# The PSUM bank of the gate's spatial mix in a hybrid decoder trunk: from the bank pair `pt` to the bank `tq`

## The chip, the cores and the metric

The kernel runs on one core of one Trainium2 chip. The metric is device time in microseconds (us) of one execution of the whole program, median of several runs. The core has five engines with a queue of instructions each: TensorE (PE in the profile; PEld is its weight load), VectorE (DVE), ScalarE (ACT), GpSimd (POOL) and SyncE (SP), which here only issues the transfers between device memory and the on-chip memory. Each engine runs its queue in order and waits at an instruction whose inputs or whose output buffer are not ready. TensorE writes its results into PSUM, a memory of eight banks of 512 float32 columns by 128 partitions; VectorE and ScalarE read them from there.

## The reference, cut to what matters

Two residual layers over 1024 tokens of width 1024. Layer 0 mixes the tokens with a spatial gate (A) and a dilated attention (B) side by side; layer 1 uses a gated linear attention; both end with a gated MLP. The change touches the gate of layer 0:

```
def chunked_gmlp(u, v, ln_g, ln_b, w_s, b_s):
    Bn, S, _ = u.shape
    nc = S // A_CHUNK                       # chunks of 128 tokens
    vn = layer_norm(v, ln_g, ln_b).reshape(Bn, nc, A_CHUNK, A_GROUPS, A_GROUP_DIM)
    causal = jnp.tril(jnp.ones((A_CHUNK, A_CHUNK), dtype=bool))
    ws = jnp.where(causal[None], w_s.astype(jnp.float32), 0.0)
    mixed = jnp.einsum('gts,bnsgc->bntgc', ws, vn) + b_s.astype(jnp.float32).T[:, :, None]
    return u.astype(jnp.float32) * mixed.reshape(Bn, S, A_WIDTH)

    # in even_mixer, h the normed input, z = h @ w_in split into u, v, q, k, vb
    a_out = chunked_gmlp(gelu(u), gelu(v), a_ln_g, a_ln_b, a_ws, a_bs)
    # b_out: three dilated attention branches of 8 heads over q, k, vb
    return concatenate([a_out, b_out], -1) @ w_out
```

## The kernel before

The 1024 tokens are eight tiles of 128. Every large product is made of float32r matmuls of 128x512, each value split into a high and a low part and three of the four partial products taken, so that one output tile of 128 tokens by 512 columns costs 8 x 3 = 24 matmuls (`mm_tok`, line 183, `PASSES`, line 41).

Layer 0 runs as follows. For each of four pairs of heads, `project` (line 776) makes queries, keys and values, and `unit` (line 750) makes one block of attention: scores on TensorE into the bank tag `sc` (line 741), mask and row minimum on VectorE (line 746), exp on ScalarE (line 747), transposes of the probabilities on TensorE into the tag `pt` (line 761, tiles `pP`), a copy to `pT` on ScalarE or VectorE (lines 764 and 766), and the product with the values into the tag `po` (line 769). `project` also transposes keys and queries into the tag `tq` (lines 821 to 828, tiles `tk` and `tq`). `dilated` (line 850) makes eight units per pair (tiles `sc3d`, `pP3d`, `po3d` for the last pair). `combine` and `combined` (lines 867 to 892) join the branches and write the result to device memory (`bcat`), after a round trip of the dilated part through device memory (`od`, then `on`).

After the last pair, `gmlp` (line 656) projects v (tiles `pv0` to `pv7`, lines 698 and 651) into two tiles `mx0` and `mx1` of four token tiles each, applies gelu (line 676) and layer norm (lines 679 to 688), and mixes along the tokens: for each half and each pair of groups one PSUM tile `pm` gets two float32 matmuls of 128x256 (line 692), and VectorE adds the bias while it moves `pm` back into `mx` (line 694). There are eight such tiles, `pm00` to `pm06` and `pm10` to `pm16`. `u_proj` (line 701) projects u (tiles `pu0` to `pu7`), applies gelu on ScalarE (line 705) and multiplies the result into `mx` (line 706). While `pu7` is made, before the matmuls of its last two slices, `turn` (line 714) transposes the first token tile for the output projection, four blocks of `mx0` and four of `cat00`, which is read back from `bcat` (line 711); the transposes go into two `pt` tiles `pc00` and `pc01` (line 720), from which ScalarE and VectorE make the two parts of `hq` (lines 101, 102). The output projection (`out_first`, line 446, tiles `po00`, `po01`, ...) reads `hq` and weights `wo`, split on ScalarE and VectorE (lines 101, 102). The second token tile is transposed at line 456 (`pc10`, `pc11`).

The eight banks of this stage are given out by tag (line 526): `pt` 2, `sc` 2, `pj` 2 (the projections), `po` 1, `tq` 1. The tiles of a tag take its banks in turn, in the order in which the program asks for them; a tile waits until the tile that held its bank has been read.

The order in each queue is not the program's: a scheduler (`schedule_with_timeline_sim`, line 1380) sorts the instructions of each engine by its own estimate of times, within the data and buffer dependencies. A handful of instructions are pinned (`keep_in_program_order`), among them the first transpose of `turn` and the first step of `combine`. The change of a bank therefore moves instructions on every engine.

Of the kernel before, what the change touches and what calls it, by code (L numbers as in the profile page):

```python
# [9 lines left out]
F32 = mybir.dt.float32  # L10
# [9 lines left out]
P = 128  # L20
# [27 lines left out]
def flat(t):  # L48
    return t.rearrange("p a b -> p (a b)")
# [7 lines left out]
def trunk(ctx: ExitStack, tc: tile.TileContext, a, out):  # L57
# [72 lines left out]
    def load_half(src, name, gains=None):  # L130

        return [w for kp in range(4)
                for w in load_w(src[kp], f"{name}{kp}", gains=None if gains is None else gains[:, 2 * kp : 2 * kp + 2])]
# [4 lines left out]
    def inv_rms(ssq, cols, n, name, r=None):  # L138
        if r is None:
            r = small.tile([P, cols], F32, tag="rs%d" % cols, name=name)  # L140
        G.tensor_scalar(r, ssq, 1.0 / n, EPS, op0=ALU.mult, op1=ALU.add)  # L141
        G.tensor_tensor(r, r, mhalf[:, :cols], op=ALU.pow)
        return r
# [506 lines left out]
    def proj512(ps, ws, name, consume, amid=None):  # L650
        for n in range(NT):
            pj = ps.tile([P, 512], F32, tag="pj", name=f"{name}{n}")
            mm_tok([(pj, slice(0, 512))], lambda k: tok(n, k), lambda k: ws[k], KD, amid if n == NT - 1 else None)
            consume(n, pj)

    def gmlp(ps, gm):

        wv = load_half(a["w_vu"][0], "wv", g0)
        lnG = gm.tile([P, 512], F32, name="lnG")
        Q.dma_start(lnG, a["ln_g"].partition_broadcast(P))  # L660
        lnB = gm.tile([P, 512], F32, name="lnB")
        Q.dma_start(lnB, a["ln_b"].partition_broadcast(P))
        bs = gm.tile([P, GROUPS], F32, name="bs")
        Q.dma_start(bs, a["a_bs"])
        ws = gm.tile([P, GROUPS, P], F32, name="ws")
        Q.dma_start(ws, a["a_ws"])

        G.affine_select(out=ws, in_=ws, compare_op=ALU.is_ge, fill=0.0, base=0,
                        pattern=[[0, GROUPS], [1, P]], channel_multiplier=-1)

        def consume(n, pj):
            half, j = n // 4, n % 4
            A.activation(mx[half][:, j, :], pj, AF.Copy, scale=r0[:, n : n + 1])
            if j < 3:
                return
            ge = A.activation(flat(mx[half]), flat(mx[half]), AF.Gelu)
            if half:
                tc.keep_in_program_order(ge)
            for j in range(4):
                gv = mx[half][:, j, :]  # L680
                st = small.tile([P, 6], F32, tag="bn", name=f"bn{half}{j}")
                V.bn_stats(st, gv)
                mv = small.tile([P, 2], F32, tag="mv", name=f"mv{half}{j}")
                V.bn_aggr(mv, st)
                r = inv_rms(mv[:, 1:2], 1, 1, f"lr{half}{j}")
                V.tensor_scalar(gv, gv, mv[:, 0:1], r, op0=ALU.subtract, op1=ALU.mult)
                V.tensor_mul(gv, gv, lnG)
                V.tensor_add(gv, gv, lnB)
            for g in range(0, GROUPS, 2):
                pm = ps.tile([P, 2, 4, 64], F32, tag="pt", name=f"pm{half}{g}")  # L690
                for i in range(2):
                    T.matmul(pm[:, i], ws[:, g + i, :], mx[half][:, :, (g + i) * 64 : (g + i) * 64 + 64],
                             start=True, stop=True)
                V.tensor_tensor(mx[half][:, :, g * 64 : g * 64 + 128].rearrange("p n (i c) -> p i n c", i=2), pm,
                                bs[:, g : g + 2, None, None].to_broadcast([P, 2, 4, 64]), op=ALU.add)

        mx = [gm.tile([P, 4, 512], F32, name=f"mx{h}") for h in range(2)]
        proj512(ps, wv, "pv", consume)
        return [mx[n // 4][:, n % 4, :] for n in range(NT)]

# [224 lines left out]
    def odd(ps, narrow, rl):  # L925

        with tc.tile_pool(name="T", bufs=1, reuse_waits="tile") as tp, \
                tc.tile_pool(name="gl", bufs=2, reuse_waits="tile") as gl:
            return gla(ps, narrow, gl, [tp.tile([P, 2, 4, 512], F32R, name=f"Tm{i}") for i in range(3)], rl)
# [284 lines left out]
    def banks(st, **bufs):  # L1214
        return Tagged({t: st.enter_context(tc.tile_pool(name="psf_" + t, bufs=b, space=PSUM, reuse_waits="tile"))
                       for t, b in bufs.items()})

    def narrow():
        pss.close()
        return banks(pss, m1=5, pt=3)  # L1220
# [4 lines left out]
    ps = banks(pss, mm=3, pt=2)  # L1225
    for l in range(2):
        w_out = a["od_w_out" if l else "ev_w_out"]
        x_in = (lambda n: x2[n]) if l else (lambda n: rows(a["x"], n))
        with ExitStack() as ops:
            if l == 1:  # L1230
                ps, last = odd(ps, narrow, ops.enter_context(tc.tile_pool(name="rl", bufs=1, side="right", reuse_waits="tile")))
# [29 lines left out]
        with tc.tile_pool(name=f"T{l}", bufs=1, reuse_waits="tile") as tp:  # L1261
            T3 = [tp.tile([P, 2, 4, 512], F32R, name=f"T{l}{i}") for i in range(3)]
            if l == 0:
                ps = narrow()
# [4 lines left out]
        ps = banks(pss, mm=3, pt=2)  # L1269
# [114 lines left out]
```

## Time and profile before

| what | value |
|---|---|
| median of 3 runs | 2152.41 us (2152.16 to 2153.36) |
| the profiled execution's own time | 2150.36 us |
| its span, first to last instruction | 2147.9 us |
| TensorE matmul busy | 2120.8 us, 99% of the span |
| VectorE, ScalarE, GpSimd busy | 1512.2, 1035.8, 478.8 us |
| mean granted TensorE clock | 0.999 |
| first and last matmul of `pm` | 333.6 and 358.8 us |
| first and last VectorE step of line 694 | 334.6 and 359.5 us |

The profile is of one execution. A row of the timeline gives the start in us, how long the group of instructions lasted, the engine, the line of the kernel, the operation, the tile it writes and the tiles it reads, how many there were, and in brackets how long the engine had been idle and what ended that. Matmul ends are modelled, so rows of TensorE overlap by a fraction of a microsecond; the chain of waits cuts the same time into pieces that don't overlap (start, length, engine, line, count). TensorE's busy time leaves 27 us of the span; a change that moves nothing but waits can win at most that, and what lies in a stretch of lowered clock.

### The profile page before, as it was taken

The numbers are of one execution on the slowest core, as the hardware profiler recorded it, in microseconds if no ns is written. First come the engines' busy times: TensorE is split into PE (matmuls) and PEld (weight loads), VectorE is DVE, ScalarE is ACT, GpSimd is POOL, SyncE is SP. The second block draws the span as 40 slices with busy tenths as digits, with TensorE's granted clock in tenths as the row PEclk, the third lists the DMA queues.
The fourth block names the chain that finished last, engine by engine and source line by source line (L and its number), as shares of the span: only waits on it lengthen the run. The fifth ranks groups of instructions, "written<-read, shape, count | busy, mean of one in ns | idle before, by whom it ended". The sixth has DMA issues, their size and how long they took to land.

```text
span 2147.9 us, 29582 instructions
## 1 busy us (share of the span) xinstructions
PE 2120.8 (99%) x10380; PEld 1797.3 (84%) x10380; DVE 1512.2 (70%) x2436; ACT 1035.8 (48%) x2014; POOL 478.8 (22%) x521
## 2 busy tenths in 40 slices
PE   8999999999999999999999999999999999999999
PEld 7999987878888888878889888888788888888887
DVE  7466654576978878655576877677788888785554
ACT  7555664264444444444454455535544444444443
POOL 6344310013424335000020011011234324220000
PEclk9999999999999999999999999999999999999999
DMA  7022313754444544765553233386555544458664
GB/s 274 25 75 68 114 45 109 250 197 148 157 167 162 167 149 155 253 238 195 199 188 123 73 107 99 132 306 212 177 167 162 169 150 156 163 172 290 214 217 165
DMA packets 159701, 353.69 MB, mean 165 GB/s; under 512 B 17424, under 2 KB 54544, under 8 KB 159168
## 3 DMA queue, kind: packets, MB, share of 16 engines
q1 hardware_dynamic: 159408, 351.68, 48.6%
q8 instruction: 81, 1.33, 0.3%
q14 instruction: 68, 0.56, 0.1%
q10 hardware_dynamic: 144, 0.13, 0.0%
HBM read 243.15 MB, written 108.59 MB: 164 GB/s over the span
## 4 chain that ended last, share of the span: by engine, by line
PE 87%; DVE 4%; DMA 3%; ACT 3%; issue 1%; POOL 0%; SPq 0%; DVEq 0%; ACTq 0%
PE pgB L293 11%; PE puB L293 11%; PE pv L193 6%; PE pgC L293 6%; PE puC L293 6%; PE pdB L405 5%; PE pj L193 5%; PE pdC L405 5%; PE po L193 4%; PE pdO L405 4%; PE puA L293 3%; PE pgA L293 3%; PE pdP L405 2%; PE pdQ L405 2%; PE pu L193 2%; PE pBq L1084 2%
## 5 line engine op out<-in xcount | busy, mean ns | idle before, releaser
L102 DVE TENSOR_TENSOR da<-ar,da 128x512 fp32r<-128x512 f32 x154 | 106.2, 690 | 155.6 <-ACT da L101 155.3
L101 ACT CAST da<-ar 128x512 fp32r<-128x512 f32 x154 | 95.9, 623 | 212.5 <-PE pdC L405 98.5
L193 PE MATMUL po<-wo,hq 128*128 128x512 f32 x768 | 185.1, 397 | 1.5 <-DVE hq L102 1.2
L193 PEld LDWEIGHTS po<-wo,hq 128*128 128x128 f32 x768 | 142.7, 189 | 31.8 <-DVE hq L102 2.4
L193 PE MATMUL pv<-wv,hq 128*128 128x512 f32 (+2 forms) x768 | 140.0, 339 | 0.0
L405 PE MATMUL pdB<-dw,da 128*128 128x512 f32 x528 | 135.5, 391 | 1.3 <-ACT u L310 0.7
L405 PE MATMUL pdC<-dw,da 128*128 128x512 f32 x528 | 135.1, 390 | 0.0
L193 PEld LDWEIGHTS pv<-wv,hq 128*128 128x128 f32 x768 | 119.1, 189 | 14.7
L193 PE MATMUL pj<-wq,hq 128*128 128x384 f32 x576 | 118.5, 344 | 0.0
L405 PEld LDWEIGHTS pdB<-dw,da 128*128 128x128 f32 x528 | 98.7, 188 | 22.7 <-ACT u L310 1.1
L405 PEld LDWEIGHTS pdC<-dw,da 128*128 128x128 f32 x528 | 99.0, 188 | 20.5
L102 DVE TENSOR_TENSOR dw<-wr,dw 128x512 fp32r<-128x512 f32 x154 | 105.6, 686 | 10.2 <-ACT dw L101 9.7
L259 POOL TENSOR_TENSOR S1g<-rg 128x512 f32<-128x512 f32 x20 | 29.4, 1468 | 373.6 <-DMA wsd<-D 262.4
L141 POOL TENSOR_SCALAR rn<-ssq 128x1 f32<-128x1 f32 x24 | 9.3, 389 | 447.2 <-ACT h L149 244.1
L405 PE MATMUL pdO<-dw,da 128*128 128x512 f32 x396 | 102.2, 389 | 0.2 <-DVE dw L102 0.2
L101 ACT CAST dw<-wr 128x512 fp32r<-128x512 f32 x154 | 95.0, 617 | 11.4 <-DMA wr<-in_w_dn 6.7
L193 PEld LDWEIGHTS pj<-wq,hq 128*128 128x128 f32 x576 | 98.2, 188 | 0.2
L405 PEld LDWEIGHTS pdO<-dw,da 128*128 128x128 f32 x396 | 74.2, 188 | 16.0 <-DVE dw L102 0.6
L324 DVE SCALAR_TENSOR_TENSOR t<-g,cw,t 128x1022 f32<-128x1022 f32 x44 | 73.8, 1677 | 0.1
L308 DVE TENSOR_TENSOR g<-g,s1g 128x512 f32<-128x512 f32 x22 | 15.2, 693 | 79.9 <-ACT s1g L307 79.9
L323 DVE SCALAR_TENSOR_TENSOR t<-g,cw,t 128x1023 f32<-128x1023 f32 x44 | 56.2, 1278 | 16.1 <-ACT t L322 16.1
L259 POOL TENSOR_TENSOR S4u<-ru,S2u 128x512 f32<-128x512 f32 x20 | 48.9, 2447 | 54.6 <-DVE wg2p L102 9.6
(1084 smaller groups left out, 5410.3 us busy)
## 6 DMA issues: line engine op xcount, KB each, us to landing
ar<-actd SPq DMA_DIRECT2D x70, 512.0 KB, 3.6
rd<-in_w_down SPq DMA_DIRECT2D x44, 512.0 KB, 3.7
wsd<-D SPq DMA_DIRECT2D x88, 256.0 KB, 2.6
rg<-in_w_gate SPq DMA_DIRECT2D x42, 512.0 KB, 3.7
ru<-in_w_up SPq DMA_DIRECT2D x42, 512.0 KB, 4.8
wr<-wsd SPq DMA_DIRECT2D x40, 512.0 KB, 4.5
actd<-t SPq DMA_DIRECT2D x66, 256.0 KB, 2.3
wr<-in_w_dn SPq DMA_DIRECT2D x30, 512.0 KB, 4.7
```

What stands on the lines that cost most here:

```text
L101: (hi or A.copy)(dst[0], src)
L102: (lo or V.tensor_sub)(dst[1], src, f32(dst[0]))
L141: G.tensor_scalar(r, ssq, 1.0 / n, EPS, op0=ALU.mult, op1=ALU.add)
L193: T.matmul(o, L[i], R[jj][:, sl], start=(k == 0 and (ii, jj) == PASSES[0]), stop=(k == nk - 1 and (ii, jj) == PASSES[-1]))
L259: G.tensor_tensor(sums[name], x, y, op=op)
L293: mm = T.matmul(o, L[ii][:, j * P : j * P + P], right[p][:, jj, j, :], skip_group_check=more, start=(not more and j == 0 and (ii, jj) == P ...
L308: V.tensor_add(C22, C22, s1)
L323: V.scalar_tensor_tensor(t[:, 1:], g[:, : S - 1], w(1), t[:, 1:], op0=ALU.mult, op1=ALU.add)
L324: V.scalar_tensor_tensor(t[:, 2:], g[:, : S - 2], w(0), t[:, 2:], op0=ALU.mult, op1=ALU.add)
L405: T.matmul(o, L[ii][:, t * P : t * P + P], R[jj], skip_group_check=more, start=start and not more and (ii, jj) == PASSES[0], stop=stop and ...
L1084: T.matmul(o, L[ii][:, j * P : j * P + P], right[p][:, jj, j, :], skip_group_check=more, start=(not more and j == 0 and (ii, jj) == PASSES ...
```

## The change

The PSUM tile `pm` of the spatial mix is asked for under the tag `tq` (one bank) instead of `pt` (two banks). Nothing else in the text changes; the same matmuls and VectorE steps run.

```
             for g in range(0, GROUPS, 2):
-                pm = ps.tile([P, 2, 4, 64], F32, tag="pt", name=f"pm{half}{g}")
+                pm = ps.tile([P, 2, 4, 64], F32, tag="tq", name=f"pm{half}{g}")
                 for i in range(2):
                     T.matmul(pm[:, i], ws[:, g + i, :], mx[half][:, :, (g + i) * 64 : (g + i) * 64 + 64],
                              start=True, stop=True)
```

In `pt` the first `pm` comes behind the `pP` tiles of all attention units, since they were asked for earlier. In `tq` it comes behind the last `tq` tile of the last `project`. The order on each engine changes as follows; numbers behind a tile's name tell apart tiles of one name.

TensorE, in the projection of v (`pv6`, `pv7`) between the units of the last pair:

```order
 L193 MATMUL pv6_4109<-wv2_0_3871,hq01_86 128x512 x3
+L692 MATMUL pm00_4041<-mx0_3894,ws_3891 128x256 x2
 L193 MATMUL pv6_4109<-wv2_1_3874,hq11_88 128x512 x3
 L193 MATMUL pv6_4109<-wv3_0_3879,hq01_86 128x512 x3
 L193 MATMUL pv6_4109<-wv3_1_3882,hq11_88 128x512 x3
 L193 MATMUL pv7_4135<-wv0_0_3855,hq01_86 128x512 x3
```

`pm00` stood in the projection `pu4`, behind the transposes of the last unit; now it stands in `pv6`, six projections earlier, between two units. The other seven follow one by one, the last, `pm16`, in `pu4` (before: in `pu7`). The last unit's product with the values (`po3d1`) now has seven tiles `pm` ahead of it instead of one, and eight matmuls of `pu4` instead of 23.

TensorE, at the end of the projection of u and the start of the output projection:

```order
 L720 MATMUL pc00_4501<-ident_73,mx0_3894 128x128 x2
-L193 MATMUL pu7_4482<-wu3_0_4244,hq01_86 128x512 x3
-L193 MATMUL pu7_4482<-wu3_1_4247,hq11_88 128x512 x3
 L720 MATMUL pc00_4501<-ident_73,cat00_4450 128x128 x2
 L720 MATMUL pc01_4508<-ident_73,mx0_3894 128x128 x2
 L720 MATMUL pc01_4508<-ident_73,cat00_4450 128x128 x2
-L456 MATMUL pc10_4581<-ident_73,mx0_3894 128x128 x2
-L456 MATMUL pc10_4581<-ident_73,cat01_4577 128x128 x2
-L456 MATMUL pc11_4588<-ident_73,mx0_3894 128x128 x2
-L456 MATMUL pc11_4588<-ident_73,cat01_4577 128x128 x2
+L193 MATMUL pu7_4482<-wu3_0_4244,hq01_86 128x512 x3
+L193 MATMUL pu7_4482<-wu3_1_4247,hq11_88 128x512 x3
```

The last six matmuls of `pu7` moved behind all eight transposes of `turn`, and the eight transposes of the second token tile moved away from here, into the last matmuls of `po00`.

VectorE, at the end of `combined` and the splits of the output weights `wo`:

```order
 L891 TENSOR_TENSOR ot3n0_3073<-ot3n0_3073,on30_3849 128x4x128
 L891 TENSOR_TENSOR ot3n4_3376<-ot3n4_3376,on31_3851 128x4x128
-L694 TENSOR_TENSOR mx1_3895<-pm14_4210,bs_3889 128x2x4x64
+L706 TENSOR_TENSOR mx1_3895<-mx1_3895,ut5_4447 128x512
+L706 TENSOR_TENSOR mx1_3895<-mx1_3895,ut6_4479 128x512
 L102 TENSOR_TENSOR wo00_0_4547<-wo00r_4545,wo00_0_4547 128x512
 L102 TENSOR_TENSOR wo00_1_4550<-wo00r_4545,wo00_1_4550 128x512
-L694 TENSOR_TENSOR mx1_3895<-pm16_4214,bs_3889 128x2x4x64
 L102 TENSOR_TENSOR wo01_0_4555<-wo01r_4553,wo01_0_4555 128x512
-L706 TENSOR_TENSOR mx1_3895<-mx1_3895,ut4_4419 128x512
-L706 TENSOR_TENSOR mx1_3895<-mx1_3895,ut5_4447 128x512
-L706 TENSOR_TENSOR mx1_3895<-mx1_3895,ut6_4479 128x512
```

No step of line 694 is left behind the first step of `combine`; of the gate's products (line 706) three instead of four stand behind `combined`, two of them ahead of the splits. On ScalarE the number of table loads is the same. On SP two transfers behind the first four of `cat` change places (`wo13r` and `cat03`), nothing else.

More of the change, by code (lines that the diff above doesn't have):

```diff
@@ L689, in consume @@
             for g in range(0, GROUPS, 2):
-                pm = ps.tile([P, 2, 4, 64], F32, tag="pt", name=f"pm{half}{g}")
+                pm = ps.tile([P, 2, 4, 64], F32, tag="tq", name=f"pm{half}{g}")
                 for i in range(2):
```

## The prediction

> **What bounds the kernel now.** I read the page first.
>
> ```profile
> span 2147.9 us, 29582 instructions
> PE 2120.8 (99%) x10380; PEld 1797.3 (84%) x10380; DVE 1512.2 (70%) x2436; ACT 1035.8 (48%) x2014; POOL 478.8 (22%) x521
> ```
>
> TensorE is busy all but 27.1 us of the span, so the change, which removes no matmul, can win only TensorE's waits and its slow matmuls. The second view is the list of TensorE's waits, for the stage that the change touches.
>
> ```profile
> PE pc L456 <- DMA cat<-bcat: 1.3, 1, 1.3
> PE po L193 <- DVE hq L102: 1.2, 1, 1.2
> PE pP3d L761 <- ACT sm3d L747: 0.6, 1, 0.6
> PE pc L720 <- DMA cat<-bcat: 0.2, 1, 0.2
> ```
>
> Third, TensorE's timeline shows where they lie: one in the attention units of the last pair, three in a row between the projection of u and the output projection.
>
> ```profile
> 322.18 0.44 PE L761 MATMUL pP3d<-ident,sm3d 128*128 128x128 f32 x2 [0.60 <-ACT sm3d L747]
> ...
> 360.84 0.38 PE L720 MATMUL pc<-ident,mx 128*128 128x128 f32 x2
> 360.98 1.64 PE L193 MATMUL pu<-wu,hq 128*128 128x512 f32 x6
> 362.87 0.44 PE L720 MATMUL pc<-ident,cat 128*128 128x128 f32 x2 [0.25 <-DMA cat<-bcat]
> ...
> 365.22 0.44 PE L456 MATMUL pc<-ident,cat 128*128 128x128 f32 x2 [1.26 <-DMA cat<-bcat]
> ...
> 367.33 7.31 PE L193 MATMUL po<-wo,hq 128*128 128x512 f32 x24 [1.24 <-DVE hq L102]
> ```
>
> The last row holds more than a wait: the first 24 matmuls of the output projection take 7.31 us. The chain of waits has the eight transposes of the next token tile (0.87 us) and the next 24 matmuls, and the table of stretches has the granted clock (columns: stretch, length, busy time and count of PE, PEld, DVE, ACT, POOL, then PEclk, DMA share, GB/s).
>
> ```profile
> 374.64 0.87 PE pc L456 x8
> 375.52 5.49 PE po L193 x24
> ```
> ```profile
> 364.00:366.00 2.00, 0.78 (x6) 0.64 (x6) 2.00 (x5) 1.18 (x3) 0.00 (x0) 1.00 0.78 273
> 366.00:367.00 1.00, 0.09 (x1) 0.00 (x0) 1.00 (x3) 0.77 (x2) 0.00 (x0) 1.00 0.94 266
> 368.00:369.00 1.00, 1.00 (x3) 0.74 (x3) 1.00 (x2) 0.00 (x0) 0.00 (x0) 0.50 1.04 426
> 371.00:372.00 1.00, 1.00 (x6) 0.81 (x6) 0.00 (x0) 0.00 (x0) 0.00 (x0) 1.00 1.00 410
> ```
>
> TensorE did 0.87 us of work in the 3 us from 364 to 367; then its clock stood at 0.50 and three matmuls instead of six fitted into 1 us. So this stage loses 0.60 + 0.25 + 1.26 + 1.24 = 3.35 us in waits and 7.31 - 5.49 = 1.82 us at half clock, 5.17 us together. VectorE is full from 364 to 367 (2.00 of 2.00, 1.00 of 1.00): a queue of work stands there, and `hq`, for which the output projection waits, is at its end.
>
> **The change part by part.** Removed and added work: none. The same 16 matmuls and 8 VectorE steps run, at the same price. What changes is where they stand, and four things follow.
>
> (1) The wait of 0.60 us. ScalarE did two table loads and a gelu between the two exps of one unit:
>
> ```profile
> 318.23 1.28 ACT L705 ACT_TABLE_LOAD   x1
> 319.52 0.69 ACT L705 ACTIVATE ut<-pu,r 128x512 f32<-128x512 f32 x1
> 320.23 1.28 ACT L747 ACT_TABLE_LOAD   x1
> ```
>
> 1.28 + 0.69 + 1.28 = 3.25 us. In the new order of ScalarE this unit's two exps stand side by side ahead of `ut1`. Another unit, the last, now has table load, `ut2`, table load between its exps; TensorE has there a `po3d` product, six and more matmuls and a `pm` in between. I take 0 for it and 0.6 us, the old wait, as the upper bound. Gain 0.60, low end 0.
>
> (2) The transfer `cat`. It ends a chain that starts with the last attention product, and whether TensorE waits for it depends on both.
>
> ```profile
> 339.53 1.78 PE pm L692 x8
> ```
>
> Two `pm` are eight pieces on TensorE; one costs 1.78 / 2 = 0.89 us, one 512-wide matmul 5.49 / 24 = 0.229 us. The last `po3d` product has six more `pm` ahead of it (+5.34) and 15 fewer matmuls (-3.43), and the wait of (1) is gone (-0.60): it comes 1.3 us later. From there the chain runs through every engine:
>
> ```profile
> 339.57 0.59 ACT L861 COPY ot3d<-po3d 128x512 f32<-128x512 f32 x1 [5.16 <-PE po3d L769]
> ```
> ```profile
> 342.45 1.34 SPq L901 DMA_DIRECT2D on<-od  x2
> ```
> ```profile
> on<-od SPq DMA_DIRECT2D x2, 264.0 KB, 3.2
> ```
> ```profile
> 347.31 1.29 DVE L706 TENSOR_TENSOR mx<-mx,ut 128x512 f32<-128x512 f32 x2
> 348.52 0.68 DVE L694 TENSOR_TENSOR mx<-pm,bs 128x512 f32<-128x512 f32 x1
> 349.12 0.15 DVE L872 TENSOR_TENSOR cM<-ot3n,on 128x8 f32<-128x8 f32 x1
> 349.19 1.28 DVE L706 TENSOR_TENSOR mx<-mx,ut 128x512 f32<-128x512 f32 x2
> 350.39 0.16 DVE L875 TENSOR_TENSOR cE<-cM,ot3n 128x8 f32<-128x8 f32 x1
> ...
> 354.75 0.68 DVE L694 TENSOR_TENSOR mx<-pm,bs 128x512 f32<-128x512 f32 x1
> ```
>
> The first `on` has landed at about 342.45 + 3.2 = 345.65 us, yet `combine` (L872) starts at 349.12: 3.5 us behind the gate's steps in VectorE's queue, then 1.2 us more for two products between L872 and L875, and 0.6 us for one step of L694 inside `combined`. In the new order these stand ahead of the chain, at times when VectorE has nothing else, or behind it. The chain then goes 5.3 us faster and starts 1.3 us later; I take off another 0.5 us, since the second `on` lands 1 us behind the first and its half of L872 waits for it. Before, `cat` was there at 362.87 us (TensorE's wait ends); now at 362.87 - 5.3 + 1.3 + 0.5 = 359.4 us. TensorE comes to its first transpose of `cat` at 360.84 - 0.60 + 2 x 0.11 = 360.5 us (0.87 / 8 = 0.11 a transpose), as the same `pm` and `pu` matmuls are behind it. The cover is thus 1.1 us, and it has to hold, because the last six matmuls of `pu7`, which hid 1.4 us of that wait before, now stand behind it. The second token tile (`pc1`), whose wait was the 1.26 us, is now transposed behind 19 matmuls of `po00`, 4.4 us after its start. Gain 0.25 + 1.26 = 1.51; with the chain as long as before the wait comes back (first rival).
>
> (3) The wait for `hq`. VectorE reached it late:
>
> ```profile
> 366.60 2.47 DVE L102 TENSOR_TENSOR hq<-pc,hq 128x512 fp32r<-128x512 f32 x4
> ```
>
> In the new order the queue ahead of `hq` is one step of L706 and six splits of `wo` after `pu6` ends, some 0.7 + 7 x 0.6 = 4.9 us, each step at its distance in that queue (four steps of `hq` in 2.47 us); TensorE meanwhile does the 24 matmuls of `pu7` and eight transposes, 5.5 + 0.9 = 6.4 us. One step of `hq` later, at 5.6 us, `po00` may start: 0.8 us of cover. Gain 1.24; low end 0.4 less.
>
> (4) The half clock. It followed 3 us with 0.87 us of matmuls; with (2) and (3) gone TensorE has no such stretch. Gain 1.82, all or nothing. [...]
>
> (5) One bank instead of two. The next `pm` may be written only when L694 has read the last one:
>
> ```profile
> L694 DVE TENSOR_TENSOR mx<-pm,bs x8: 676/687/692, 334.6 to 359.5; 128x512 f32<-128x512 f32 x8
> ```
>
> Side by side, eight tiles in one bank would cost up to 7 x 0.69 = 4.8 us of waiting. But in the new order at least ten 512-wide matmuls stand between two `pm`, 2.3 us and more. I take 0. [...]
>
> Sum: 0.60 + 1.51 + 1.24 + 1.82 = 5.17 us. The profiled execution took 2150.36 us (span 2147.9 and 2.5 around it), 2.05 below the median of the runs; a gain of whole waits carries over to the median: 2152.41 - 5.17 = 2147.2 us. Against the low ends (0.6 and 0.4 less) it is 2148.2.
>
> What is late next: the stage behind waits again, the two longest times here:
>
> ```profile
> 437.72 1.53 PE L163 MATMUL pt<-ident,xt 128*128 128x128 f32 x12 [0.65 <-DVE xt L153]
> 470.95 2.79 PE L293 MATMUL pgB<-hq,wg0p 128*128 128x512 f32 x11 [1.31 <-DVE hq L102]
> ```
>
> These hang on VectorE and transfers that start from the third tile of the output projection, so they should move forward with it.
>
> **The rivals.** *A, the transfer chain is not shorter.* If `cat` takes as long as before (339.57 to 362.87, 23.3 us) from a start 1.3 us later, it is there at 364.2 us; TensorE, which now has nothing else to do, waits 3.7 us, does six transposes and six matmuls (0.65 + 1.37) and starts `po00` at 366.2 instead of 367.33, but with the eight transposes of `pc1` (0.87) still to do. Gain 0.3 us, or 2.1 with full clock: 2150.3 to 2152.1. For it: it is the longest chain here, and my cover is 1.1 us; against: the VectorE rows that leave it.
>
> *B, the half clock stays*, because something else made it or because a wait that is left is enough for it. Gain 3.35: 2149.1 us. For it: nothing in the rows; against: it follows the three waits at once. [...]
>
> *C, the gain is given back.* The two rows above wait for VectorE. If its work and the transfers there keep their own time, these waits grow by what was won: 2152.4 us. Against it: that work starts from TensorE's results in the output projection.
>
> *D, slower: the one bank stops TensorE.* The place is `pm14` in `pu3`. Its bank is freed by L694 of `pm12`, on VectorE behind the product with `ut2` (L706), which ScalarE makes between table loads. Fifteen matmuls of 512 columns stand between `pm12` and `pm14`, 3.4 us, less 0.69 for L694 itself: 2.7 us of slack. Each further microsecond stops TensorE, and the last unit with it; beyond 2.7 + 5.17 = 7.9 us of delay the kernel is slower than before, and beyond 12 us by over 0.2%. The nearest rows are those of (1): a load, a gelu and a load in the way are 3.25 us, which would cost 0.6 us. Four such delays would be needed: 2153 to 2157 us.
>
> **How the numbers follow.** The whole gain: 0.60. A: 0.20; B: 0.06; C: 0.09; D: 0.05. A change of 0.2% is 4.3 us, about what a measurement of this kernel can tell from none. The whole gain passes it if no more than 0.9 us of new waits comes with it; I give that nine in ten: faster 0.54. A, B, C and the rest of the first make 0.41 within 0.2%; D makes 0.05. The range holds the first case with its bounds (1.2 us to the far side for waits further on that shrink too), B and most of A: 2146.0 to 2152.0. The likeliest case alone: 2146.0 to 2148.6.
>
> **What would show it.** Right: no wait over 0.3 us for `cat` or `hq` between 355 and 370 us; PEclk at 1.00 through the first 24 `po` matmuls, which then last about 5.5 us apart from the transposes among them; L872 within 1 us of the landing of `on`; `po00` starting near 362.5 us. Wrong: a wait of `pc00` for `cat` of over 1 us (A), PEclk at 0.50 near 365 us without it (B), waits of over 3 us between 430 and 485 us (C), a wait of `pm` for L694 (D).

## The result and the profile after

| kernel | median, us | runs |
|---|---|---|
| before, measured beside it | 2152.90 (2150.25 to 2154.76) | 8 |
| after | 2146.55 (2145.40 to 2150.18) | 8 |

The ratio is 0.9975, interval 0.9965 to 0.9986: some 5.4 us less (3.0 to 7.5), where 5.17 were forecast. The ratio is not the quotient of the two medians, which is 0.9971, 6.35 us less. The profiled execution of after took 2149.18 us (span 2146.4), second longest of its eight runs. One execution of the third measurement of after, below, took 2979.05 us at a granted clock of 0.665, and every number given leaves it out.

The page of after has the same work in it as the page of before.

```profile
span 2146.4 us, 29574 instructions
PE 2121.5 (99%) x10380; PEld 1798.0 (84%) x10380; DVE 1516.1 (71%) x2436; ACT 1036.4 (48%) x2014; POOL 481.1 (22%) x521
```

The times of two executions, counted from the span's start, can't be set side by side: something ahead of the change already differs. So I use a mark that the change doesn't move, the product `po3n`, which in after stands shortly ahead of the first `pm`, and a second one, the start of the long run of `po` matmuls behind the last `pc`. First TensorE's timeline of before:

```profile
290.26 1.00 PE L769 MATMUL po3n<-vN,pT3n 128*128 128x64 f32 x8
...
375.27 5.73 PE L193 MATMUL po<-wo,hq 128*128 128x512 f32 x24
...
407.53 29.55 PE L193 MATMUL po<-wo,hq 128*128 128x512 f32 x128
...
479.33 1.09 PE L163 MATMUL pt<-ident,xt 128*128 128x128 f32 x8 [0.38 <-DVE xt L153]
```

Then the same view of after, with the places that the prediction spoke of:

```profile
291.98 1.00 PE L769 MATMUL po3n<-vN,pT3n 128*128 128x64 f32 x8
...
361.57 0.38 PE L720 MATMUL pc<-ident,mx 128*128 128x128 f32 x2
361.79 0.38 PE L720 MATMUL pc<-ident,cat 128*128 128x128 f32 x2
...
363.84 4.57 PE L193 MATMUL po<-wo,hq 128*128 128x512 f32 x19
...
403.37 10.71 PE L193 MATMUL po<-wo,hq 128*128 128x512 f32 x46
414.31 1.81 PE L193 MATMUL po<-wo,hq 128*128 128x512 f32 x4 [0.24 <-DVE xh L443]
416.44 18.47 PE L193 MATMUL po<-wo,hq 128*128 128x512 f32 x78 [0.31 <-DVE wo L102]
434.85 1.53 PE L163 MATMUL pt<-ident,xt 128*128 128x128 f32 x12
...
468.06 2.79 PE L293 MATMUL pgB<-hq,wg0p 128*128 128x512 f32 x11 [1.29 <-DVE hq L102]
476.97 1.09 PE L163 MATMUL pt<-ident,xt 128*128 128x128 f32 x8 [0.91 <-DVE xt L153]
```

No row of TensorE's matmuls between the two marks has a bracket any more: the waits for `sm3d`, for `cat` (twice) and for `hq` are gone. The stage between the marks takes 407.53 - 290.26 = 117.27 us before and 403.37 - 291.98 = 111.39 us after, so 5.88 us less. The table of stretches says what this is made of, first for before, then for after, over exactly this stage. The row of before has TensorE's columns alone (stretch, length, PE busy and count, then PEclk, DMA share, GB/s); the row of after has all engines between.

```profile
290.26:407.53 117.27, 113.92 (x581) 0.99 0.39 127
```
```profile
291.98:403.37 111.39, 111.39 (x581) 94.44 (x579) 61.65 (x134) 54.75 (x94) 7.15 (x10) 1.00 0.40 131
```

The same 581 matmuls. Before, TensorE was idle for 117.27 - 113.92 = 3.35 us of the stage, which is the prediction's 0.60 + 0.25 + 1.26 + 1.24 to the hundredth; after, it is idle for nothing. The other 113.92 - 111.39 = 2.53 us are busy time that has become shorter: 1.82 of it was forecast as half clock. In after the clock stands at 1.00 through the whole stage, and TensorE is full.

VectorE's timeline of after shows `combine` waiting for its data, where before the data waited for VectorE. SP's queue shows when `cat` is issued, first in after, then in before:

```profile
347.80 0.17 DVE L872 TENSOR_TENSOR cM<-ot3n,on 128x8 f32<-128x8 f32 x1 [3.27 <-DMA on<-od]
...
351.38 2.14 DVE L889 TENSOR_TENSOR on<-on,cE 128x512 f32<-128x512 f32 x2
353.44 2.13 DVE L891 TENSOR_TENSOR ot3n<-ot3n,on 128x512 f32<-128x512 f32 x2
```
```profile
357.63 0.33 SPq L711 DMA_DIRECT2D cat<-bcat  x1
```
```profile
359.83 0.33 SPq L711 DMA_DIRECT2D cat<-bcat  x1
```

In after, ScalarE's timeline shows when the last `po3d` is copied, and the timeline of TensorE's weight loads (PEld) a short wait for `hq` that no matmul shows:

```profile
342.23 0.59 ACT L861 COPY ot3d<-po3d 128x512 f32<-128x512 f32 x1 [1.98 <-PE po3d L769]
```
```profile
363.77 4.21 PEld L193 LDWEIGHTS po<-wo,hq 128*128 128x128 f32 x19 [0.21 <-DVE hq L102]
```

### The profile page after: what moved, and what is told of

It is laid out like the page before. It is cut to its first block, busy times and chain, and to the rows that moved or that the text cites. A ratio compares the mean times of both kernels' runs of the same rounds, so it can differ in the third digit from the quotient of the medians.

```text
span 2146.4 us, 29574 instructions
## 1 busy us (share of the span) xinstructions
PE 2121.5 (99%) x10380; PEld 1798.0 (84%) x10380; DVE 1516.1 (71%) x2436; ACT 1036.4 (48%) x2014; POOL 481.1 (22%) x521
## 4 chain that ended last, share of the span: by engine, by line
PE 90%; DMA 3%; DVE 3%; ACT 2%; issue 1%; POOL 1%; SPq 0%; DVEq 0%; ACTq 0%
PE pgB L293 11%; PE puB L293 11%; PE pv L193 6%; PE pdB L405 6%; PE pgC L293 6%; PE puC L293 6%; PE pdC L405 6%; PE po L193 5%; PE pj L193 5%; PE pdO L405 4%; PE puA L293 3%; PE pgA L293 3%; PE pdP L405 2%; PE pdQ L405 2%; PE pu L193 2%; PE pBq L1084 2%
```

## The experiments

Every kernel was measured beside the kernel before on the same chip. For each the table gives the length of the stage between the two marks in its profiled execution, what it is shorter than 117.27 us, and what the medians say. The two columns of gains come from different executions; they agree within 1.1 us in every row but the last.

| kernel | stage, us | gain there, us | gain by the medians, us | ratio to before |
|---|---|---|---|---|
| after | 111.39 | 5.88 | 6.35 | 0.9975 [0.9965, 0.9986] |
| after, second measurement | 111.34 | 5.93 | 4.83 | 0.9978 [0.9969, 0.9987] |
| after, third | 111.38 | 5.89 | 5.92 | 0.9979 [0.9968, 0.9990] |
| only first half in `tq` | 111.35 | 5.92 | 5.71 | 0.9967 [0.9955, 0.9979] |
| the same, second measurement | 111.35 | 5.92 | 6.66 | 0.9972 [0.9963, 0.9982] |
| the same, third | 111.38 | 5.89 | 5.42 | 0.9974 [0.9964, 0.9984] |
| only second half in `tq` | 113.91 | 3.36 | 2.97 | 0.9982 [0.9973, 0.9991] |
| before, kept warm | 115.74 | 1.53 | 1.41 | 0.9990 [0.9982, 0.9999] |
| after, longer chain to `cat` | 115.91 | 1.36 | 0.95 | 0.9999 [0.9990, 1.0008] |
| before, products on GpSimd | 119.68 | -2.41 | -2.12 | 1.0010 [1.0001, 1.0019] |
| one bank, late (`po`) | 127.36 | -10.09 | -13.34 | 1.0052 [1.0040, 1.0064] |

**One bank without the early place.** The tag `po` also has one bank, but its earlier tiles are the `po3d` products up to the last one, so the `pm` come late, and into one bank, as after. They come even later than before: 54.3 to 81.9 us behind `po3n` (348.5 to 376.1, with `po3n` at 294.2), where before has 43.3 to 68.5. So this kernel changes the place as well as the number of banks.

```
-                pm = ps.tile([P, 2, 4, 64], F32, tag="tq", name=f"pm{half}{g}")
+                pm = ps.tile([P, 2, 4, 64], F32, tag="po", name=f"pm{half}{g}")
```

> The mix takes the single bank `po`, which is free only after the last attention unit: one bank as in the change, but late as before. My theory (the early place of the mix wins, by clearing VectorE's queue ahead of `combine` and `hq`): no gain, and slower than before by 1 to 8 us, since the eight tiles now also wait for each other, 0.69 us each, and `cat` and `hq` come later; half clock at the start of the output projection. Rival (the gain comes from taking the mix out of the banks `pt`, whatever the place): as the change, 4 to 6 us faster than before.

Measured: 2165.92 us beside 2152.58, slower by 0.5%. The direction was right, the size was not: 13.3 us, where 1 to 8 were expected. The half clock lay almost wholly ahead of the output projection, whose first 24 matmuls take 5.92 us. The list of TensorE's waits (us in total, times, longest) and its timeline:

```profile
PE pm L692 <- DVE mx L694: 7.0, 5, 3.1
```
```profile
356.44 1.13 PE L692 MATMUL pm<-mx,ws 128*128 128x256 f32 x4 [0.78 <-DVE mx L694]
...
374.61 2.07 PE L692 MATMUL pm<-mx,ws 128*128 128x256 f32 x4 [3.06 <-DVE mx L694]
```

Where two `pm` stand near each other, TensorE waits 0.78 us for L694 each time, a little more than the 0.69 that the prediction put on it; where VectorE has something else in front, 1.6 and 3.1 us. The four matmuls behind the longest wait take 2.07 us instead of 1.13, at half clock. In the changed kernel no `pm` waits for L694. So the single bank is no gain in itself, and it is free only where the tiles stand apart, as in the new order. How the 10.09 us lost in the stage divide between the bank and the later place isn't shown, beyond the 7.0 us of these waits.

**Each half alone.** The tag is chosen by `half`, in two kernels.

```
+                pm = ps.tile([P, 2, 4, 64], F32, tag="pt" if half else "tq", name=f"pm{half}{g}")
```
```
+                pm = ps.tile([P, 2, 4, 64], F32, tag="tq" if half else "pt", name=f"pm{half}{g}")
```

Only the first half in `tq`:

> Only the first half's four tiles use `tq`, the second half's stay in `pt`. My theory: the last `po3d` product has five tiles of the mix ahead of it instead of seven, four of the eight VectorE steps are gone from the end, and two of the last four stand ahead of `combine`; the end of the projection of u is ordered as in the change. Most or all of the gain, 3.5 to 6 us faster than before, no half clock. Rival (it takes all eight out of the way): 2 to 3 us, with a wait for `cat` left.

Only the second half in `tq`:

> Only the second half's four tiles use `tq`, the first half's stay in `pt`. My theory: the first half's VectorE steps and two products with `ut` stay ahead of and inside `combine`, so the chain to `cat` is shortened by less; TensorE waits for `cat` 0 to 2 us and may fall to half clock. 1 to 4 us faster than before. Rival (either half is as good): 5 to 6 us faster.

Measured: 2146.87 us with the first half alone, 2149.61 with the second alone, beside 2152.58. The first half does all of it: its stage takes 111.35 us, the 111.39 of the whole change, and `combine` starts as soon as `on` is there (346.75 us, 3.52 us of waiting for it). The second half alone leaves two of the four waits in TensorE's timeline, and no lowered clock:

```profile
323.82 0.44 PE L761 MATMUL pP3d<-ident,sm3d 128*128 128x128 f32 x2 [0.60 <-ACT sm3d L747]
...
366.56 0.44 PE L456 MATMUL pc<-ident,cat 128*128 128x128 f32 x2 [1.23 <-DMA cat<-bcat]
```

Its gain of 3.36 us in the stage is close to the prediction's other terms, 0.25 + 1.24 + 1.82 = 3.31. Both gains by the medians, 5.71 and 2.97 us, lie where they were expected. Once the first `pm` no longer stand behind all of the attention in `pt`, the second four find `pt` free in time, and where they go makes no difference to the stage.

**Before, kept warm.** Twenty matmuls of 128x256, whose result nobody reads, are pinned between `pc00`, `pc01` and the second tile's transposes, into a tile of the tag `sc`. This adds work to TensorE and takes away no wait's cause.

```
+            warm = [ps.tile([P, 256], F32, tag="sc", name="warm")]
+            [tc.keep_in_program_order(T.matmul(warm[0], identr, hq[0][1][:, 0, 0, :256],
+                                               start=True, stop=True)) for j in range(20)]
```

> The kernel before, with 20 matmuls of 128x256 between the transposes of `pc0` and `pc1`, whose result nobody reads: 2.3 us of TensorE work laid into the 2.5 us in which it waited. My theory (the half clock comes from the waits): the first 24 matmuls of the output projection take 5.5 us instead of 7.3, and the kernel is 1 to 2 us faster than before, in spite of the added work. [...]

Measured: 2151.17 us beside 2152.58. In TensorE's timeline the twenty matmuls fill the time of the waits, and the first 24 `po` matmuls run at full speed:

```profile
292.01 1.00 PE L769 MATMUL po3n<-vN,pT3n 128*128 128x64 f32 x8
...
365.32 2.60 PE L724 MATMUL warm<-hq,identr 128*128 128x256 f32 x20
...
369.13 5.74 PE L193 MATMUL po<-wo,hq 128*128 128x512 f32 x24 [0.33 <-DVE hq L102]
```

They start 369.13 - 292.01 = 77.12 us behind this execution's `po3n`, as before (367.33 - 290.26 = 77.07), and then take 5.74 us instead of 7.31: 1.57 us, which is the gain. So it was the thin stretch ahead, with little work on TensorE, that lowered the clock, and this part of the gain can be had without moving anything.

**A longer chain to `cat`.** The changed kernel, with one more copy of the last pair's dilated part in device memory. The copy moves 1024 x 132 values, 528 KB, in one transfer, and the loads `on` behind it are issued 4.0 us after it (345.72 and 349.73 in SP's timeline), where the expectation has 132 KB and 2.4 to 3.5 us.

```
+            if p == PAIRS - 1:
+                od2 = dram.tile([S, 132], F32, name="od2")
+                Q.dma_start(od2, od)
+                od = od2
```

> The changed kernel, with one more copy of the last pair's 132 KB in device memory (od into od2) ahead of the load on. The result is the same. The chain to cat gets longer by one transfer, some 2.4 to 3.5 us by the rows for od and on, and TensorE takes up the transposes of cat one matmul later (0.2 us). Theory (the time came from an earlier cat, with a cover of some 1.1 us and no more): TensorE waits for cat again, 1 to 2.5 us, then 1 to 1.3 us for hq, and the first 24 po matmuls run at half clock for a part (6 to 7.3 us instead of 5.5): 2 to 5 us of the gain are lost, so 2148.5 to 2152 us, a ratio to the kernel before of 0.998 to 1.000. Rival (the gain came from elsewhere, the 15 matmuls that no longer stand in po3d's way, or the wait for sm3d): cat may come 3 us later for nothing, 2146 to 2147 us, ratio 0.9975.

Measured: 2151.23 us beside 2152.18, so the gain is lost but for 0.95. The chain of waits, TensorE's timeline, and the clock behind the wait:

```profile
362.00 2.95 DMA cat<-bcat
```
```profile
364.99 1.11 PE L720 MATMUL pc<-ident,cat 128*128 128x128 f32 x4 [2.39 <-DMA cat<-bcat]
```
```profile
364.00:366.00 2.00, 1.01 (x5) 1.01 (x6) 1.28 (x3) 0.28 (x1) 0.00 (x0) 0.76 1.02 351
366.00:368.00 2.00, 2.00 (x6) 1.55 (x6) 1.64 (x3) 1.41 (x3) 0.00 (x0) 0.50 1.02 277
368.00:370.00 2.00, 2.00 (x9) 1.61 (x8) 1.28 (x3) 1.20 (x2) 0.00 (x0) 0.89 1.04 414
```

`cat` was issued at 362.00 us, 4.56 later than in after and 0.64 later than in before, each counted from its own `po3n` (291.79 here). It cost a wait of 2.39 us in a place that the scheduler had moved 1.0 us back. The wait for `hq` didn't come back, since the last five matmuls of `pu7` now cover it; that point of the expectation was wrong. The half clock did: 0.48 + 1.00 + 0.22 = 1.70 us. Together 2.39 + 1.70 = 4.09 of the 4.52 us by which the stage is longer than in after. The rival, a gain that comes from elsewhere, falls. The scheduler's order changes with this edit too, and what that alone costs isn't shown.

**The products on GpSimd.** The kernel before, with the last four products of line 706 on another engine, to take them out of VectorE's queue ahead of `hq`.

```
-            V.tensor_mul(mixed[n], mixed[n], t)
+            (G if n > 3 else V).tensor_mul(mixed[n], mixed[n], t)
```

> The kernel before, with the gate's last four products of line 706 on GpSimd instead of VectorE, so that only the wo subtractions stand ahead of hq there. Order of TensorE as before. Theory (the wait for hq, 1.24 us, is the chain from the late cat: transpose, ScalarE's cast, VectorE's subtraction): the wait for hq falls by 0.4 us at most, to 0.8 to 1.2 us, half clock stays (7 us or more for the first 24 po matmuls), 2152 to 2153 us, ratio 0.9995 to 1.001. Rival (VectorE's queue, with the products in it, makes the wait): the wait for hq falls under 0.4 us and the half clock goes with it, 2150 us, ratio 0.9985 to 0.999.

Measured: 2154.30 us beside 2152.18, slower by 0.1%, and neither theory had that. TensorE's, GpSimd's and VectorE's timelines:

```profile
369.80 7.99 PE L193 MATMUL po<-wo,hq 128*128 128x512 f32 x24 [2.74 <-DVE hq L102]
```
```profile
361.06 6.33 POOL L706 TENSOR_TENSOR mx<-mx,ut 128x512 f32<-128x512 f32 x4 [4.30 <-DVE mx L694]
```
```profile
361.32 3.28 DVE L102 TENSOR_TENSOR wo<-wo01r,wo 128x512 fp32r<-128x512 f32 x2 [0.40 <-ACT wo L101]
364.52 3.42 DVE L102 TENSOR_TENSOR wo<-wo02r,wo 128x512 fp32r<-128x512 f32 x2
367.87 1.28 DVE L102 TENSOR_TENSOR wo<-wo03r,wo 128x512 fp32r<-128x512 f32 x2
```

While GpSimd multiplied, the subtractions of `wo` on VectorE took about 1.7 us each; as soon as it had finished (361.06 + 6.33 = 367.39 us), 0.68. So `hq`, at the end of that queue, came later: the wait grew from 1.24 to 2.74 us, and the first 24 matmuls took 7.99 instead of 7.31 us, 2.2 us in all, the measured loss. My theory, that only `cat` set the wait for `hq`, falls here: with `cat` waited for 1.5 us, where it was 1.26 before, VectorE's queue alone made that wait twice as long. Whether a shorter queue would have ended it can't be told from this kernel, but the rows of before tell it. There ScalarE's part of `hq` for the first token tile stands in its timeline as

```profile
363.80 1.07 ACT L101 CAST hq<-pc 128x512 fp32r<-128x512 f32 x2
```

and is done at 364.87 us, while VectorE's steps for `hq` begin at 366.60 (the row is in the prediction), right behind other work, with no bracket. Its first two steps take 2.47 / 2 = 1.23 us; on a free VectorE they would have ended at 366.1, just when TensorE was done with its transposes (365.71 + 0.38, by its timeline). So in before, too, the queue made the wait.

**Twice more, side by side.** The first profile of after lost some 2 us behind the second mark, and the first half alone had come out with a little lower ratio than the whole change (0.9967 against 0.9975; its median was 0.32 us higher, not lower as one expectation below has it). Both kernels were measured twice more without any edit.

> The changed kernel once more, as it is, for a second profile beside its neighbours. In the first profile 128 po matmuls after 403 us took 31.5 us instead of the 29.6 us of before, with waits of 0.24 and 0.31 us for xh and wo and 4 matmuls in 1.81 us. Theory (the lead meets transfers that come at their old time): the loss is there again, 1 us or more in that stretch. Rival (this one execution's transfers): the stretch takes 29.6 to 30 us, and the lead of 5.9 us is kept to the end. Time by both 2146 to 2147.5 us, ratio 0.997 to 0.998.

> Only the first half of each pm pair in the bank tq, the second stays in pt: once more, beside the changed kernel on the same chip. Theory (the first half in tq frees the order, the second in tq adds nothing, pt being free by then too): 2146 to 2147 us, the same as the changed kernel within 0.5 us. Rival (two banks are better than one): 1 to 2 us less than the changed kernel, 2145 to 2145.5 us.

> The changed kernel a third time, for the comparison with its neighbour. In the profiled runs so far executions differ by one or two half-clock stretches between 30 and 60 us, 1.7 us each, ahead of everything the change touches. Both theories: 2146 to 2148 us, ratio 0.997 to 0.998; po00 starts 71.9 us after the product po3n.

> Only the first half of each pm pair in tq, a third time, beside the changed kernel. The two measurements so far are 0.3 and 1.8 us below the changed kernel, but po00 starts at the same 71.9 us after po3n in both. Theory (the same; the distance is early half-clock stretches that some executions have and others not): within 0.7 us of its neighbour. Rival (two banks are better by something behind 490 us): again 1 to 2 us below it.

Measured: after 2147.35 and 2146.90 us, the first half alone 2145.52 and 2147.40. The second pair differs by 1.83 us, which is what the rival had (two banks are better); the third pair differs by 0.50 us the other way, as the theory had. The difference has both signs and the stages agree to 0.05 us, so the runs don't show that two banks are better, nor exclude a small gain behind the stage. TensorE's timeline of after's second measurement:

```profile
293.11 1.00 PE L769 MATMUL po3n<-vN,pT3n 128*128 128x64 f32 x8
...
404.45 29.27 PE L193 MATMUL po<-wo,hq 128*128 128x512 f32 x128
433.95 1.53 PE L163 MATMUL pt<-ident,xt 128*128 128x128 f32 x12 [0.23 <-DVE xt L153]
...
476.39 1.09 PE L163 MATMUL pt<-ident,xt 128*128 128x128 f32 x8 [1.24 <-DVE xt L153]
```

Here the 128 `po` matmuls take 29.27 us without a wait, 29.5 us from the mark to the next transposes where the first profile had 434.85 - 403.37 = 31.5. So the waits for `xh` and `wo` and the slow matmuls from 414 us are not there in every execution of after; the theory of a standing loss falls. (A wait for `wo` of 0.15 to 0.31 us stands in this stretch of five other profiles.) Of the lead behind the second mark, one wait takes something back each time: that for `xt` before the last transposes, 0.38 us in before, 0.91, 1.24 and 1.11 in the three profiles of after. The other wait for `xt`, before the first transposes, gives some of it back: 0.65 us in before, none, 0.23 and 0.58 in after. At the last transposes, counted from `po3n` (479.33 - 290.26 in before, 476.39 - 293.11 here), 5.79 us of the lead of 5.93 are left here, 5.08 in the third profile, 4.08 in the first. The multiply ahead of the last transposes waits for a transfer, by VectorE's timeline of the same execution:

```profile
475.58 0.75 DVE L153 TENSOR_SCALAR xt<-xt,rn 128x1024 f32<-128x1024 f32 x1 [1.66 <-DMA xd<-xt]
```

## Why the prediction was right, step by step

- **(1) The wait for `sm3d`, 0.60 us.** Gone, as forecast. The second half alone still has it, so it is the four `pm` of the first half, moved forward, that reorder ScalarE there.
- **(2) `cat`, 1.51 us.** Both waits are gone. ScalarE copies the last `po3d` 342.23 - 291.98 = 50.25 us behind the mark, 0.94 later than before (339.57 - 290.26 = 49.31), where 1.3 was forecast. The chain to `cat` no longer stands in VectorE's queue, and `cat` is issued 65.65 us behind the mark (357.63 - 291.98) instead of 69.57 (359.83 - 290.26): 3.92 us earlier, where the forecast comes to 5.3 - 1.3 - 0.5 = 3.5. With the 2.95 us from issue to the end of the wait that the longer chain shows (362.00 to 364.95 in its chain of waits) it lands at about 360.6, an estimated 1.2 us before TensorE's 361.79: the cover of 1.1 us was well sized. Two terms inside were off and cancelled in part, so this closeness is in part luck: `combine` starts 347.80 - 291.98 = 55.8 us behind the mark, where the prediction comes to 345.65 + 1.3 - 290.26 = 56.7, and the pairs of steps at L889 and L891 take 2.14 and 2.13 us, where two at 0.69 us are 1.3 (their distance included). GpSimd works on its own part of L889 from 351.42 to 354.42, beside them.
- **(3) `hq`, 1.24 us.** Gone, but only just. That VectorE's queue sets it was right, by the rows of before and by the kernel with the products on GpSimd. The cover of 0.8 us was not there: the weights of the first `po00` matmul wait 0.21 us for `hq`, and its matmul follows without idle time. The same 0.21 us stand in after's other two profiles. By VectorE's timeline the splits of `wo` came every 0.68 us (360.39 to 361.75 for two), where 0.6 was counted, and this used up most of the cover. That nothing of the wait was left was partly luck.
- **(4) The half clock, 1.82 us.** Gone with the waits, and it goes without any move when the gap is filled (1.57 us). The thin stretch was the cause: TensorE was busy for 1.10 of the 3.41 us ahead of the fall (last section), and no single wait there was over 1.26 us. Only one execution of before was profiled, so it isn't shown that its clock falls in each one.
- **(5) One bank, cost 0.** Right in this order; with the tag `po`, where tiles stand near each other, 0.78 us a tile and more.
- **The sum, 5.17 us.** The stage gave 5.88: the 3.35 us of waits, forecast to the hundredth, and 2.53 us of busy time. The half clock was sized a little too large. By the clock it makes 1.70 us (last section), not 1.82: the prediction took a length from the chain of waits (5.49) off one from the timeline (7.31), where rows of TensorE overlap; the timeline's own row for the next 24 matmuls is 5.73, which leaves 1.58. The other 2.53 - 1.70 = 0.83 us were in no term. Most of it can be read from the rows: two transposes last 0.38 us, but the next row stands 0.22 us behind them (361.57 and 361.79 in after), and in front of a wait nothing lies over this end of 0.16 us. In front of the wait of 0.25 us stand six matmuls, 1.64 us long and 6 x 0.229 = 1.37 apart, 0.27 us. With 0.16 for the other three this is an estimated 0.75 us of the 0.83. It isn't the whole account: in the stretch with a single wait, from `po3n` to the first `pc`, TensorE was busy for 69.98 us in before and 69.59 in after, with 364 matmuls each. That is 0.39 us for one wait, in a changed order, and the part beyond 0.16 isn't explained. So the sum came near because one term was too large and a missing one outweighed it.
- **What comes behind.** The wait for `hq` at 470.95 us moved along, as forecast (1.29 instead of 1.31). The second one for `xt` grew by 0.5 to 0.9 us and the first one shrank by 0.1 to 0.7; outside the first profile this leaves 0.1 to 0.8 us less lead, so rival C holds for a small part of the gain.
- **The rivals.** A (a chain no shorter) gave 2150.3 to 2152.1 us, and the kernel with a longer chain measured 2151.23, through the wait and half clock that A described; the changed kernel isn't in that case. B (the half clock stays) didn't happen, and the warm kernel, with one profile, speaks against another cause than the thin stretch. D's mechanism exists and was measured, but not in the changed order.

## What to carry to other kernels

In this program a tile waits for the earlier tiles of its tag, so choosing a bank is choosing a place in the order: look for the tag whose earlier tiles are finished when the data is ready, and ask only then how many banks it has. Count matmuls and busy time between two marks that the change doesn't touch; the difference then splits into idle time and slow work, and the span's noise stays out. A gap in front of a long run of matmuls can cost more than its own length: in before the clock fell behind the gaps, which cost 1.70 us more. A cover worked out to some 1 us may not be there: of the two here one held and one was used up.

## What the runs showed that was not expected

**The clock fell for 3.4 us at a time.** The tables of stretches of before and then of the kernel with the products on GpSimd:

```profile
366.00:368.00 2.00, 0.76 (x3) 0.56 (x3) 2.00 (x5) 0.77 (x2) 0.00 (x0) 0.89 0.89 295
368.00:370.00 2.00, 2.00 (x6) 1.51 (x6) 1.07 (x2) 0.00 (x0) 0.00 (x0) 0.50 1.02 418
370.00:372.00 2.00, 2.00 (x9) 1.61 (x8) 0.00 (x0) 0.00 (x0) 0.00 (x0) 0.76 1.03 422
```
```profile
366.00:368.00 2.00, 0.88 (x6) 0.64 (x6) 2.00 (x3) 1.07 (x2) 1.40 (x1) 0.94 0.90 293
368.00:370.00 2.00, 0.20 (x1) 0.20 (x2) 2.00 (x4) 0.00 (x0) 0.00 (x0) 0.50 0.99 383
370.00:372.00 2.00, 2.00 (x5) 1.61 (x6) 1.54 (x3) 0.00 (x0) 0.00 (x0) 0.50 1.03 422
372.00:374.00 2.00, 2.00 (x6) 1.52 (x6) 0.00 (x0) 0.00 (x0) 0.00 (x0) 0.50 1.03 414
374.00:376.00 2.00, 2.00 (x9) 1.59 (x8) 0.00 (x0) 0.00 (x0) 0.00 (x0) 0.85 0.49 193
```

What the clock lacks of 1.00, times 2 us a row, is 0.22 + 1.00 + 0.48 = 1.70 us in before, 1.70 too with the longer chain, and 0.12 + 1.00 + 1.00 + 1.00 + 0.30 = 3.42 with the products on GpSimd: one or two spells of 3.4 us at half speed. Up to the last matmul, no profile here has a part of one: in tables of 10 us a row, what the clock lacks in one place comes to 1.7 us or a multiple of it, to the rounding. The longest wait ahead of the fall was 1.26 us in before and 2.39 us with the longer chain.

How much work stood ahead can be read by taking the 3.41 us that end where a spell begins; 3.41 us is how long the clock of before stands at 0.50 (367.56 to 370.97). TensorE was busy for 1.10 us of them in before (364.15 to 367.56), for 1.02 with the longer chain (361.61 to 365.02) and for 1.15 with the products on GpSimd (364.36 to 367.77). With the second half alone it was busy for 2.18 us around its wait of 1.23 us (365.23 to 368.64), and the clock stayed. Far ahead of the change, about 2.1 us went both ways: in after's first profile the clock stood at 0.50 from 50.98 to 54.40, behind 3.41 us with 2.09 us of work (47.57 to 50.98); in before 2.08 us (46.71 to 50.12) had no fall behind them. What tells the two apart isn't shown.

**The same spells make part of the spread between executions.** Between 30 and 60 us, far ahead of the change, before's profiled execution had the clock at 1.00 throughout, and after's second one had not, as the table of stretches shows for 50 to 60 us, before first:

```profile
50.00:60.00 10.00, 9.74 (x67) 9.25 (x68) 5.58 (x16) 5.49 (x18) 5.02 (x10) 1.00 0.28 85
```
```profile
50.00:60.00 10.00, 8.62 (x49) 8.03 (x48) 6.31 (x17) 5.54 (x19) 4.29 (x9) 0.83 0.30 96
```

In the three of the twelve profiles with no spell between 30 and 60 us `po3n` came at 290.26 to 291.00 us, in the six with one at 291.47 to 292.01, with two at 292.07 and 293.11, with three at 294.21.

**VectorE beside GpSimd.** A subtraction of 128x512 took about 1.7 us instead of 0.68 while GpSimd multiplied. Four such steps, on `wo01` and `wo02`, took 3.28 + 3.42 = 6.70 us; in before the same four took 0.68 to 0.69 us each, so the price was 4 us. Why they were slower isn't shown.
